# A depthwise convolution wholly on TensorE: four taps to a pass from shifted copies, four channel groups in the array's columns

## The chip, the core and the metric

The kernel runs on one core of a Trainium2 chip. Its time is the device time of one execution in microseconds (us). A core has TensorE (PE), VectorE (DVE), ScalarE (ACT), GpSimd (POOL) and SyncE (SP), which here only issues transfers. They run side by side and wait for one another through semaphores.

## What is computed

A sequence of 256 tokens of width 1024 and a context of as many go through two layers of four mixers (attention, Fourier, convolution, pooling), each followed by a gated FFN, and then through a second block. Both streams, sequence and context, pass layer 0's mixers; of the context, layer 1 needs keys and values only. The change touches the convolution, in each layer:

```python
def conv_module(a, dw_w, dw_b, ln_g, ln_b, w_pw):
    glu = a[..., :W_CONV] * jax.nn.sigmoid(a[..., W_CONV:])
    y = lax.conv_general_dilated(
        glu, dw_w[:, None, :], window_strides=(1,),
        padding=[(CONV_WIDTH // 2, CONV_WIDTH // 2)],
        dimension_numbers=('NWC', 'WIO', 'NWC'),
        feature_group_count=W_CONV) + dw_b
    y = jax.nn.silu(layer_norm(y, ln_g, ln_b))
    return y @ w_pw
```

with `W_CONV` 256 channels and `CONV_WIDTH` 31: each channel has its own 31 taps along the tokens.

## The kernel before

Channels lie on the partitions and tokens along the rows. Weights come in pieces of 128x1024 through a ring of four `raw` tiles on SP's queue (L232). ACT rounds each to `wh` (L244), DVE takes the rest as `wl` (L246), and a product is three passes on PE: `wh` by the high and low part of the activation `A`, and `wl` by the high part (`mm3`, L274 to L276; with tokens on the output's partitions `tm`, L299 to L301). A layer's input projections go in the order c (the convolution's input, two halves of 128 channels), Q, K/V, f (Fourier), p (pooling); attention, the mixers' small products and the output projection `p_wo` follow.

The program's order comes from a cooperative scheduler, `Flow`: side work is a generator that is spawned with a delay and yields estimated durations, and each piece of the main line calls `tick` with an estimate of its own, whereupon generators that have come due emit their next instructions. A list scheduler then orders each engine but SP by its estimates; SP keeps the program's order.

After `glu` has written the gated input to `GP` (L688; 15 zero columns on each side of each stream), the 31 taps of each half are shared out. `conv_pe` does 8 on PE: eight matmuls with a diagonal 128x128 matrix, `cdg`, over shifted views of `GP`, into the PSUM tile `p_cv`. `conv_taps` does 23 on DVE: L632, then 22 at L636, and L640 adds `p_cv`. `conv_ln` (layer norm, `p_mean`, `p_pw`) waits for both halves. N is 512 columns in layer 0 (two streams) and 256 in layer 1.

`mod_bg` streams the modulation matrices of later parts: for each piece POOL copies one element to `wm` (L422, which holds the load back until `pace[0]` is there), ACT issues the load (L423), and DVE does a weighted row sum for each stream (`jg` L427, `wm` L429). It starts when both `conv_taps` are done. The first two parts are done in the prologue by `p_mod` (L464), whose stationary operand is 128x32.

In attention, `p_s` at L763 is a score matmul, L740 its row minimum on DVE, `pe` (L743) the exponentials on ACT, `p_s` at L747 the transposes of these on PE, `pT` (L749) their copies, and `p_o` (L783) the product with V. `awo` is the output of a head group; L795 rounds it to `A` on ACT, L796 takes the rest on DVE. L948 adds `p_wo` to the residual `XC`. `p_ua` is the FFN's first product, whose input L364 and L365 write.

Of the kernel before, what the change touches and what calls it, by code (L numbers as in the profile page):

```python
# [24 lines left out]
F32 = mybir.dt.float32  # L25
# [6 lines left out]
D = 1024  # L32
# [6 lines left out]
GW = T + 2 * PAD  # L39
# [6 lines left out]
NPE = 8  # L46
CVD, FOD = 0.9, 1
# [58 lines left out]
for _n, _w in (("c", 16), ("bmod0", 48), ("bmod1", 48), ("g1_0", 8), ("g1_1", 8), ("g2_0", 8),  # L106
               ("g2_1", 8), ("dw_0", 62), ("dw_1", 62), ("db_0", 2), ("db_1", 2), ("lg_0", 2), ("lg_1", 2),
               ("lb_0", 2), ("lb_1", 2), ("ps_0", 2), ("ps_1", 2), ("n1", 8), ("n2", 8), ("fg", 8), ("bs", 8)):
    PK[_n] = _o
    _o += _w  # L110
# [42 lines left out]
def tile_kernel(ctx, tc, xin, pk_d, rows_d, lc_d, bc_d, wmod0, wmod, win, wout, wfi, wfo, wsm, win2w, win2, wproj, wout2,  # L153
# [30 lines left out]
    V.memset(ones, 1.0)  # L184
    mhalf = cpool.tile([128, 12], F32, name="mhalf")
# [9 lines left out]
    G.tensor_scalar(P("dw_0", 0, 124), P("dw_0", 0, 124), 0.5, None, op0=OP.mult)  # L195
# [367 lines left out]
    for l in range(2):  # L563
# [4 lines left out]
        with ExitStack() as mctx:  # L568
# [6 lines left out]
            UP = mp.tile([128, ns, UW], F32, name="UP")  # L575
            S2 = mp.tile([128, ns, UW], F32, name="S2")
            S4 = mp.tile([128, ns, UW], F32, name="S4")
            G.memset(UP[:, :, 0:POOL_PAD], 0.0)
            G.memset(UP[:, :, POOL_PAD + T:], 0.0)
            U = mp.tile([128, 2, N], F32, name="U")  # L580
# [4 lines left out]
            QT = [mp.tile([128, 2, 256], F32, name=f"QT{s}") for s in streams]  # L585

# [20 lines left out]
            cps = {}  # L607

            def conv_diag(f):

                w = lpool.tile([128, D], F32, tag="wm", name="cdg", bufs=WMB)
                for j in range(NPE):
                    tap = pk[:, PK[f"dw_{l}"] + f * TAPS + j:PK[f"dw_{l}"] + f * TAPS + j + 1]
                    if l == 0:
                        G.tensor_scalar(w[:, 128 * j:128 * j + 128], ident, tap, None, op0=OP.mult)
                    else:
                        S.activation(w[:, 128 * j:128 * j + 128], ident, AF.Copy, scale=tap)
                return w

            def conv_pe(f, w):  # L620

                cps[f] = psm("p_cv")
                for j in range(NPE):
                    PE.matmul(cps[f][:, :N].rearrange("p (s t) -> p s t", t=T), w[:, 128 * j:128 * j + 128],
                              GP[:, f, :, j:j + T], start=j == 0, stop=j == NPE - 1)
                    tick(0.0017 * N)

            def conv_taps(f, delay):
                y = Y[:, f].rearrange("p (s t) -> p s t", t=T)
                dw = PK[f"dw_{l}"] + f * TAPS  # L630
                per = 0.35 * ns
                V.tensor_scalar(y, GP[:, f, :, NPE:NPE + T], pk[:, dw + NPE:dw + NPE + 1], P(f"db_{l}", f), op0=OP.mult,  # L632
                                op1=OP.add)
                yield per + delay
                for j in range(NPE + 1, TAPS):
                    V.scalar_tensor_tensor(y, GP[:, f, :, j:j + T], pk[:, dw + j:dw + j + 1], y, op0=OP.mult, op1=OP.add)  # L636
                    yield per + delay
                while f not in cps:
                    yield 0.3
                V.tensor_tensor(Y[:, f], cps[f][:, :N], Y[:, f], op=OP.add)  # L640
                yield per
                G.tensor_copy(snap, Y[:, f, 0:1])
                pace[0] = snap
# [3 lines left out]
            def conv_ln(t0, t1):  # L647

                yield from wait(t0, t1)
# [86 lines left out]
            def att_unit(s, t, i, j, pT, sums, sp):  # L736
                nk = 4 if s == 0 else 2
                W = 128 * nk
                st = wk.tile([128, 1], F32, tag="ast", name="ast", bufs=4)
                V.tensor_reduce(st, sp[:, :W], axis=AX.X, op=OP.min)  # L740
                yield 0.8
                pe = mp.tile([128, 512], F32, tag="pe", name="pe", bufs=PEB)
                S.activation(pe[:, :W], sp[:, :W], AF.Exp, bias=st, scale=-1.0, accum_out=sums[:, j:j + 1])  # L743
                yield 0.9
                tp = sp
                for kt in range(nk):
                    PE.transpose(tp[:, 128 * kt:128 * kt + 128], pe[:, 128 * kt:128 * kt + 128], ident)  # L747
                yield 0.6
                S.copy(pT[:, :W], tp[:, :W])  # L749
                yield 0.5  # L750

            def attention(s, deps):
                yield from wait(*deps)
                nk = 4 if s == 0 else 2
                for t in range(2):
                    for i in range(2):
                        pts, us = [], []
                        sums = wk.tile([128, 2], F32, tag="asum", name="asum", bufs=4)

                        sps = [psm("p_s") for _ in range(2)]  # L760
                        for j in range(2):
                            pr = slice(64 * j, 64 * j + 64)
                            PE.matmul(sps[j][:, :128 * nk], QT[s][pr, t, 128 * i:128 * i + 128], KTt[pr, :128 * nk],  # L763
                                      start=True, stop=True)
                        yield 0.22 * nk + 0.2
                        for j in range(2):
                            pT = mp.tile([128, 512], F32, tag="PT", name="pT", bufs=PTB)
# [75 lines left out]

            PY = S2[:, :, POOL_PAD:POOL_PAD + T]

            def pool_f(f):
# [14 lines left out]
            def poolmix(f, d):  # L861
                yield d
                p = pmm("p_pl")
                PE.matmul(p[:, :N].rearrange("p (s t) -> p s t", t=T), sm[:, 1024 + 128 * f:1024 + 128 * f + 128], PY,
# [51 lines left out]
            for f in range(2):  # L916
                conv_pe(f, cdg[f])
# [539 lines left out]
def _pack(inp):  # L1457
# [9 lines left out]
    for l in range(2):  # L1467
# [3 lines left out]
        put(f"dw_{l}", inp["conv_dw_w"][l].reshape(TAPS, 2, 128).transpose(2, 1, 0).reshape(128, 2 * TAPS))  # L1471
# [79 lines left out]
```

## Time and profile before

| | us |
|---|---|
| median of 3 runs | 1340.57 (1340.22 to 1340.75) |
| the profiled execution | 1341.05 |
| its span | 1339.3 |

| engine | busy us | share of the span |
|---|---|---|
| PE | 1300.0 | 97% |
| DVE | 931.9 | 70% |
| ACT | 621.4 | 46% |
| POOL | 256.7 | 19% |

The span runs from the first to the last recorded instruction of the profiled execution; its own time is 1.75 us longer, and 0.48 us above the median. A matmul of f32 data shows as two records. Where it says fp32r, or where the operands are `wh`, `wl` and `A`, a matmul is one record. A record's duration includes the pipeline, so the spacing of starts tells what a matmul costs in a row of them. In the rows below, "128\*32" is the size of the stationary operand, "<-" stands between output and inputs, a bracket gives the idle time before an instruction and what ended it, and PEld is PE's weight loading.

### The profile page before, as it was taken

The page shows a single profiled execution, that of the slowest core. Times are in us where ns is not written, and L with a number is a line of the kernel's source. Part 1 is how long each engine was busy: PE and PEld are TensorE (multiplying, and loading weights), DVE is VectorE, ACT ScalarE, POOL GpSimd, SP SyncE. Part 2 cuts the span into 40 slices and gives each one's busy share as a digit, 9 for nine tenths or more (in the row PEclk, how much of TensorE's full clock was granted, in tenths as well). Part 3 has the DMA queues.
Part 4 walks back from the last instruction along what each step waited for, and adds up shares of the span by engine and source line. Part 5 has one row for each costly group of instructions (what it writes and reads, how often), then busy time and mean ns, then how long its engine had stood idle before and what let it go on. Part 6 is the DMA issues. An engine that isn't in the chain of part 4 may idle for free.

```text
span 1339.3 us, 20667 instructions
## 1 busy us (share of the span) xinstructions
PE 1300.0 (97%) x7764; PEld 1107.6 (83%) x7764; DVE 931.9 (70%) x1658; ACT 621.4 (46%) x1045; POOL 256.7 (19%) x310
## 2 busy tenths in 40 slices
PE   5999989899999999999999999999999999999997
PEld 4786569788888888899789999888788889888886
DVE  3697997999883333359667666657675777888754
ACT  4434534322132222245565554445675655655542
POOL 4134543243310000133420000010110002211100
PEclk9999999999999999999999999999999999999999
DMA  9624453677883222334135554675344344555463
GB/s 370 221 79 149 134 173 99 244 250 245 300 299 119 95 86 65 102 130 145 45 106 191 178 187 152 189 259 185 129 147 157 135 160 171 191 190 186 154 190 102
DMA packets 66612, 224.67 MB, mean 168 GB/s; under 512 B 7504, under 2 KB 8656, under 8 KB 66384
## 3 DMA queue, kind: packets, MB, share of 16 engines
q1 hardware_dynamic: 53968, 179.21, 39.8%
q10 hardware_dynamic: 12080, 42.50, 9.5%
q0 software_dynamic: 464, 1.64, 0.3%
q8 instruction: 61, 1.00, 0.3%
q14 instruction: 39, 0.32, 0.1%
HBM read 222.27 MB, written 1.05 MB: 167 GB/s over the span
## 4 chain that ended last, share of the span: by engine, by line
PE 87%; DVE 5%; DMA 2%; ACT 2%; issue 2%; POOL 1%; POOLq 0%; SPq 0%; DVEq 0%; ACTq 0%
PE p_dn L283 6%; PE p_ua L275 5%; PE p_ua L276 5%; PE p_ua L274 4%; PE p_ug L276 4%; PE p_ug L275 4%; PE p_ug L274 4%; PE p_ga L283 3%; PE p_gg L283 3%; PE p_dn L274 3%; PE p_dn L275 3%; PE p_dn L284 3%; PE p_dn L276 3%; PE p_gt L283 2%; PE p_wo L276 2%; PE p_wo L275 2%
## 5 line engine op out<-in xcount | busy, mean ns | idle before, releaser
L246 DVE TENSOR_TENSOR wl<-raw,wh 128x1024 fp32r<-128x1024 f32 (+2 forms) x340 | 393.6, 1159 | 249.2 <-ACT wh L244 247.7
L244 ACT CAST wh<-raw 128x1024 fp32r<-128x1024 f32 (+1 forms) x344 | 333.8, 974 | 317.9 <-PE p_ug L275 86.6
L339 POOL TENSOR_TENSOR ss<-ss,sq 128x256 f32<-128x256 f32 (+1 forms) x43 | 45.3, 1054 | 441.5 <-ACT sq L338 295.1
L275 PE MATMUL p_ua<-A,wh 128*128 128x258 f32 (+2 forms) x368 | 122.3, 332 | 3.5 <-DVE A L365 3.5
L283 PE MATMUL p_dn<-H,wh 128*128 128x512 f32 x352 | 124.1, 397 | 0.0
L276 PE MATMUL p_ug<-A,wl 128*128 128x258 f32 (+2 forms) x368 | 122.3, 332 | 0.0
L276 PE MATMUL p_ua<-A,wl 128*128 128x258 f32 (+2 forms) x368 | 122.1, 332 | 0.0
L275 PE MATMUL p_ug<-A,wh 128*128 128x258 f32 (+2 forms) x368 | 121.9, 331 | 0.0
L274 PE MATMUL p_ua<-A,wh 128*128 128x258 f32 (+2 forms) x368 | 121.6, 331 | 0.0
L274 PE MATMUL p_ug<-A,wh 128*128 128x258 f32 (+2 forms) x368 | 121.6, 331 | 0.0
L429 DVE SCALAR_TENSOR_TENSOR wm<-wm,scb 128x1024 f32<-128x1024 f32 x80 | 98.2, 1232 | 10.8 <-DMA wm<-in_wmod 10.7
L284 PE MATMUL p_dn<-H,wl 128*128 128x256 f32 x352 | 98.5, 281 | 0.0
L283 PEld LDWEIGHTS p_dn<-H,wh 128*128 128x128 f32 x352 | 66.0, 188 | 16.1
L275 PEld LDWEIGHTS p_ua<-A,wh 128*128 128x128 f32 x368 | 69.4, 189 | 11.0 <-DVE A L365 3.9
L275 PEld LDWEIGHTS p_ug<-A,wh 128*128 128x128 f32 x368 | 69.5, 189 | 7.2
L276 PEld LDWEIGHTS p_ua<-A,wl 128*128 128x128 f32 x368 | 69.5, 189 | 6.9
L274 PEld LDWEIGHTS p_ug<-A,wh 128*128 128x128 f32 x368 | 69.3, 188 | 7.0
L274 PEld LDWEIGHTS p_ua<-A,wh 128*128 128x128 f32 x368 | 69.3, 188 | 7.0
L276 PEld LDWEIGHTS p_ug<-A,wl 128*128 128x128 f32 x368 | 69.4, 189 | 6.9
L274 PE MATMUL p_dn<-H,wh 128*128 128x512 f32 (+1 forms) x198 | 72.4, 367 | 0.0
L275 PE MATMUL p_dn<-H,wh 128*128 128x512 f32 (+1 forms) x198 | 72.4, 366 | 0.0
L276 PE MATMUL p_dn<-H,wl 128*128 128x512 f32 (+1 forms) x198 | 72.4, 366 | 0.0
(380 smaller groups left out, 3130.4 us busy)
## 6 DMA issues: line engine op xcount, KB each, us to landing
raw<-in_wfi SPq DMA_DIRECT2D x88, 512.0 KB, 3.8
wm<-in_wmod ACTq DMA_DIRECT2D x80, 512.0 KB, 4.5
raw<-in_win SPq DMA_DIRECT2D x44, 512.0 KB, 3.8
raw<-in_wgu SPq DMA_DIRECT2D x44, 512.0 KB, 3.7
raw<-in_win2w SPq DMA_DIRECT2D x40, 512.0 KB, 4.0
raw<-in_wout SPq DMA_DIRECT2D x24, 512.0 KB, 3.7
raw<-in_wfo SPq DMA_DIRECT2D x32, 384.0 KB, 3.1
raw<-in_wfo SPq DMA_DIRECT2D x32, 320.0 KB, 3.2
```

The costliest lines, as they stand in the source:

```text
L244: S.copy(h[:, :n], raw[:, :n])
L246: (G if every and j % every == 0 else V).tensor_tensor(lo[:, :n], raw[:, :n], h[:, :n].bitcast(F32), op=OP.subtract)
L274: PE.matmul(ps, w[0], a[:, 0], start=first, stop=False, **kw)
L275: PE.matmul(ps, w[0], a[:, 1], start=False, stop=False, **kw)
L276: ins = PE.matmul(ps, w[1], a[:, 0], start=False, stop=last, **kw)
L283: PE.matmul(p.rearrange("p (h n) -> p h n", h=2), w[0], a, start=first, stop=False)
L284: PE.matmul(p[:, 0:256], w[1], a[:, 0], start=False, stop=last)
L339: (eng or G).tensor_tensor(ss[0][:, cs], ss[0][:, cs], sq[:, :n], op=OP.add)
L429: V.scalar_tensor_tensor(w, w, 1.0, scb[:, 0], op0=OP.mult, op1=OP.mult, accum_out=modv[:, l, part, 0, k:k + 1])
```

## The change

All taps go to PE, with a 32nd tap of zero. `conv_shift` copies each group of 32 channels of `GP` four times, shifted by 0 to 3 columns, to the four quarters of the partitions of `GS` (16 transfers a half, 32 a layer, 32 partitions by one or two streams by 284 columns each). A matmul with a 128x32 stationary matrix then adds four taps of 32 channels at once. `conv` does eight such passes for each of the four groups, 64 matmuls a layer; the four groups of a pass write the four quarters of `p_cv`'s partitions. ACT evacuates a half with the bias. `conv` is a generator, spawned 8.0 estimated us after `glu`; before, `conv_pe` stood on the main line behind K/V. `cdg` is now one broadcast product on POOL for each half. `mod_bg` waits for nothing any more; its first pieces are paced by `GP`. The tiles of the pooling mixer and of the exponentials (`UP`, `S2`, `S4`, `U`, `pe`, `pT`) are allocated when the convolution has been emitted, in the place of `GS`. Line numbers in the changed kernel are 3 higher up to the convolution; `p_cv` stands at L627, the copies at L618, and `jg` and `wm` at L430 and L432.

```diff
-NPE = 8
-CVD, FOD = 0.9, 1
+CVS = 8.0
+FOD = 1
...
+    id32 = cpool.tile([128, 32], F32, name="id32")
+    V.tensor_reduce(id32, ident.rearrange("p (g c) -> p c g", c=32), axis=AX.X, op=OP.add)
...
             def conv_diag(f):
-                w = lpool.tile([128, D], F32, tag="wm", name="cdg", bufs=WMB)
-                for j in range(NPE):
...
+                w = lpool.tile([128, D], F32, tag="wm", name="cdg", bufs=WMB).rearrange("p (q c) -> p q c", c=32)
+                G.tensor_tensor(w, id32[:, None, :].to_broadcast([128, 32, 32]),
+                                P(f"dw_{l}", 32 * f, 32)[:, :, None].to_broadcast([128, 32, 32]), op=OP.mult)
                 return w
...
+            def conv_shift(f):
+                gs = gp.tile([128, 4, ns, SW], F32, tag="GS", name="GS", bufs=2)
+                for g in range(4):
+                    for j in range(4):
+                        SP.dma_start(gs[32 * j:32 * j + 32, g], GP[32 * g:32 * g + 32, f, :, j:j + SW])
+                return gs
+
+            def conv(gss):
+                for f in range(2):
+                    p = psm("p_cv")
+                    for j in range(8):
+                        for g in range(4):
+                            PE.matmul(p[32 * g:32 * g + 32, :N].rearrange("p (s t) -> p s t", t=T), cdg[f][:, 4 * j + g],
+                                      gss[f][:, g, :, 4 * j:4 * j + T], start=j == 0, stop=j == 7)
+                        yield 0.35 * ns
+                    yield 0.4
+                    S.activation(Y[:, f], p[:, :N], AF.Identity, bias=P(f"db_{l}", f))
+                    yield 0.6
+                G.tensor_copy(snap, Y[:, 1, 0:1])
                 pace[0] = snap
...
-            cv0 = spawn(conv_taps(0, CVD))
-            cv1 = spawn(conv_taps(1, CVD), 0.5)
-            cv = spawn(conv_ln(cv0, cv1))
+            cvm = spawn(conv([conv_shift(f) for f in range(2)]), CVS)
+            cv = spawn(conv_ln(cvm))
             if l == 0:
+                pace[0] = GP[:, 1, 0, PAD:PAD + 1]
                 spawn(mod_bg([(0, 2, True, BG0), (0, 4, True, BG0), (0, 3, True, BG0), (0, 5, True, BG1),
                               (1, 1, True, BG1), (1, 0, True, BG1), (1, 2, False, BG1), (1, 4, False, BG1),
-                              (1, 3, False, BG1), (1, 5, False, BG1)], cv0, cv1))
+                              (1, 3, False, BG1), (1, 5, False, BG1)]))
...
-            for f in range(2):
-                conv_pe(f, cdg[f])
+
+            join(cvm)
+            gctx.close()
+            ap = mctx.enter_context(tc.tile_pool(name=f"a{l}", bufs=1))
...
```

On PE in layer 0, the convolution stood between the projections to f and p; the second half, and the start of the scores behind it, read like this before (`qt` is a rotated head, `ident` the identity with which PE transposes, `QT` and `KTt` the results):

```order
L276 MATMUL p_p<-A_73,wl 128x512
L727 MATMUL p_qt<-ident,qt_894 128x128 x3
L624 MATMUL p_cv<-GP,cdg 128x512 x8
L727 MATMUL p_qt<-ident,qt_923 128x128 x3
L763 MATMUL p_s<-KTt,QT_521 128x256 x4
L747 MATMUL p_s<-ident,pe 128x128 x4
L652 MATMUL p_mean<-Y,mean_w 128x512 x2
```

After, it stands among the K/V projections; here are the end of its first half and the start of its second:

```order
L302 MATMUL p_kv<-wh,A_73 128x256
L627 MATMUL p_cv<-GS,cdg 32x512 x29
L303 MATMUL p_kv<-wl,A_73 128x256
L304 MATMUL p_kv<-wh,A_73 128x256
L302 MATMUL p_kv<-wh,A_73 128x256
L303 MATMUL p_kv<-wl,A_73 128x256
L304 MATMUL p_kv<-wh,A_73 128x256
L627 MATMUL p_cv<-GS,cdg 32x512
L302 MATMUL p_kv<-wh,A_73 128x256
L303 MATMUL p_kv<-wl,A_73 128x256
L627 MATMUL p_cv<-GS,cdg 32x512
L304 MATMUL p_kv<-wh,A_73 128x256
```

The first three matmuls of each half are scattered singly among `p_kv` (those of the first half stand before this piece), and 29 follow in one run. In layer 1 the same engine has runs of 1, 1, 1, 30, 1, 1 and 29.

Behind the second run of 29, PE goes on with the scores of the first head:

```order
L277 MATMUL p_f<-A_73,wh 128x512
L627 MATMUL p_cv<-GS,cdg 32x512 x29
L754 MATMUL p_s<-KTt,QT_517 128x256 x2
L643 MATMUL p_mean<-Y,mean_w 128x512
L278 MATMUL p_f<-A_73,wh 128x512
```

From there 16 `p_f` matmuls, the other `p_mean` and three transposes stand ahead of the transposes of `pe`, which were next to the scores before.

On DVE, behind `glu` in layer 0, the row sums of `mod_bg` stand where the taps stood. Before (`qst` and `qt` belong to the Q/K preparation):

```order
L699 TENSOR_REDUCE qst<-qsq 128x6
L636 SCALAR_TENSOR_TENSOR Y<-GP,pk,Y 128x512 x2
L721 TENSOR_TENSOR qt_809<-QK_518,rows 128x256
L721 TENSOR_TENSOR qt_809<-QK_518,rows 128x128
L699 TENSOR_REDUCE qst<-qsq 128x6
L636 SCALAR_TENSOR_TENSOR Y<-GP,pk,Y 128x512 x2
L721 TENSOR_TENSOR qt_843<-QK_518,rows 128x256
```

and now:

```order
L690 TENSOR_REDUCE qst<-qsq 128x6
L432 SCALAR_TENSOR_TENSOR wm,modv<-wm,scb 128x1024
L712 TENSOR_TENSOR qt_891<-QK_514,rows 128x256
L712 TENSOR_TENSOR qt_891<-QK_514,rows 128x128
L690 TENSOR_REDUCE qst<-qsq 128x6
L430 SCALAR_TENSOR_TENSOR jg,modv<-wm,scb 128x1024
L712 TENSOR_TENSOR qt_936<-QK_514,rows 128x256
```

The Q/K preparation keeps its place among them; the tap operations are gone and the row sums, which came after the convolution, stand between its steps.

## Rows read from the trace of the kernel before

**Rows 1.** Page, busy time of each engine, share of the span, instructions
```profile
PE 1300.0 (97%) x7764; PEld 1107.6 (83%) x7764; DVE 931.9 (70%) x1658; ACT 621.4 (46%) x1045; POOL 256.7 (19%) x310
```

**Rows 2.** Page, the chain that ended last, shares of the span
```profile
PE 87%; DVE 5%; DMA 2%; ACT 2%; issue 2%; POOL 1%; POOLq 0%; SPq 0%; DVEq 0%; ACTq 0%
```

**Rows 3.** Stretches: length; busy PE, PEld, DVE, ACT, POOL; clock, DMA share, GB/s
```profile
56.60:112.70 56.10, 56.09 (x314) 44.81 (x314) 49.97 (x79) 15.63 (x33) 22.51 (x18) 1.00 0.25 81
112.70:195.30 82.60, 75.93 (x392) 49.63 (x391) 78.48 (x153) 42.18 (x103) 37.30 (x42) 0.98 0.55 179
...
593.70:646.50 52.80, 52.74 (x409) 51.12 (x409) 51.40 (x107) 25.96 (x56) 17.91 (x21) 1.00 0.40 132
646.50:696.80 50.30, 46.66 (x344) 38.48 (x344) 29.66 (x57) 32.31 (x69) 18.48 (x19) 1.00 0.21 68
```

**Rows 4.** Waits of PE, 50 to 260 us: total us, times, longest
```profile
PE p_ua L275 <- DVE A L365: 3.5, 2, 2.1
PE p_s L747 <- ACT pe L743: 1.9, 1, 1.9
PE p_wo L274 <- ACT A L795: 1.1, 1, 1.1
PE p_wo L274 <- DVE XC L948: 1.0, 1, 1.0
PE p_wo L275 <- DVE A L796: 1.0, 1, 1.0
```

**Rows 5.** Waits of PE, 585 to 720 us
```profile
PE p_s L763 <- DVE Y L640: 1.2, 1, 1.2
...
PE p_o L783 <- ACT pT L749: 1.0, 1, 1.0
```

**Rows 6.** Groups of instructions, DVE taps of layer 0: busy us, mean ns | idle
```profile
L636 DVE SCALAR_TENSOR_TENSOR Y<-GP,pk,Y 128x512 f32<-128x512 f32 x44 | 31.4, 753 | 0.0
```

**Rows 7.** Timeline of PE: start, duration in us, instruction
```profile
105.87 7.04 PE L624 MATMUL p_cv<-GP,cdg 128*128 128x512 f32 x16
112.75 0.49 PE L727 MATMUL p_qt<-ident,qt 128*128 128x128 f32 x3
```

**Rows 8.** Groups of instructions, convolution matmuls of layer 1
```profile
L624 PE MATMUL p_cv<-GP,cdg 128*128 128x256 f32 x32 | 7.2, 379 | 0.0
```

**Rows 9.** Timeline of PE around one modulation piece of the prologue
```profile
33.32 0.39 PE L275 MATMUL p_c<-A,wh 128*128 128x512 f32 x1
33.55 0.39 PE L276 MATMUL p_c<-A,wl 128*128 128x512 f32 x1
33.87 1.93 PE L464 MATMUL p_mod<-rawm,scf 128*32 128x256 f32 x32
35.74 0.50 PE L274 MATMUL p_c<-A,wh 128*128 128x512 f32 x1
36.08 0.39 PE L275 MATMUL p_c<-A,wh 128*128 128x512 f32 x1
```

**Rows 10.** Timeline of SP's DMA issues
```profile
50.42 0.33 SPq L571 DMA_DIRECT2D sm<-in_wsm  x1
51.87 7.57 SPq L232 DMA_DIRECT2D raw<-in_win  x4
```

**Rows 11.** Timeline of DVE, second half of `GP` in layer 0
```profile
59.47 0.68 DVE L688 SCALAR_TENSOR_TENSOR GP<-sg,p_c 128x512 f32<-128x512 f32 x1
```

**Rows 12.** DMA issues: size, median us from issue to landing
```profile
pk<-in_pk SPq DMA_DIRECT2D x1, 8.0 KB, 2.0
```

**Rows 13.** Stretch of attention, line 427 alone: DVE busy, clock, DMA share, GB/s
```profile
112.70:195.30 82.60, 28.93 (x44) 0.98 0.55 179
```

**Rows 14.** Timeline of DVE in the tail of layer 0's attention
```profile
190.65 1.22 DVE L427 SCALAR_TENSOR_TENSOR jg<-wm,scb 128x1024 f32<-128x1024 f32 x1
...
191.80 0.29 DVE L796 TENSOR_TENSOR A<-awo,A 128x128 fp32r<-128x128 f32 x1
```

**Rows 15.** Groups of instructions, weight loads of the convolution matmuls
```profile
L624 PEld LDWEIGHTS p_cv<-GP,cdg 128*128 128x128 f32 x64 | 11.7, 189 | 7.0 <-issue 6.3
```

More of the change, by code (lines that the diff above doesn't have):

```diff
@@ L38 @@
 PAD = 15
-GW = T + 2 * PAD
+GW = T + 2 * PAD + 1
+SW = T + 28
 POOL_PAD = 8
@@ L106 @@
 for _n, _w in (("c", 16), ("bmod0", 48), ("bmod1", 48), ("g1_0", 8), ("g1_1", 8), ("g2_0", 8),
-               ("g2_1", 8), ("dw_0", 62), ("dw_1", 62), ("db_0", 2), ("db_1", 2), ("lg_0", 2), ("lg_1", 2),
+               ("g2_1", 8), ("dw_0", 64), ("dw_1", 64), ("db_0", 2), ("db_1", 2), ("lg_0", 2), ("lg_1", 2),
                ("lb_0", 2), ("lb_1", 2), ("ps_0", 2), ("ps_1", 2), ("n1", 8), ("n2", 8), ("fg", 8), ("bs", 8)):
@@ L192, in P @@
         return pk[:, PK[name] + i:PK[name] + i + n]
-    G.tensor_scalar(P("dw_0", 0, 124), P("dw_0", 0, 124), 0.5, None, op0=OP.mult)
+    G.tensor_scalar(P("dw_0", 0, 128), P("dw_0", 0, 128), 0.5, None, op0=OP.mult)
     seq = []
@@ L574, in tile_kernel @@
             G.memset(GP[:, :, :, PAD + T:], 0.0)
[L575 to L580, printed above, removed]
             Y = mp.tile([128, 2, N], F32, name="Y")
@@ L585, in tile_kernel @@
             QT = [mp.tile([128, 2, 256], F32, name=f"QT{s}") for s in streams]
+            gctx = mctx.enter_context(ExitStack())
+            gp = gctx.enter_context(tc.tile_pool(name=f"g{l}", bufs=1))
             CG = mp.tile([128, 2, 2, 64], F32, name="CG")
@@ L606, in tile_kernel @@
             acc = {}
-            cps = {}
             def conv_diag(f):
-                w = lpool.tile([128, D], F32, tag="wm", name="cdg", bufs=WMB)
-                for j in range(NPE):
[L613 to L617, printed above, removed]
-                return w
@@ L620, in conv_pe @@
[L620 to L642, printed above, removed]
+                w = lpool.tile([128, D], F32, tag="wm", name="cdg", bufs=WMB).rearrange("p (q c) -> p q c", c=32)
@@ L643, in conv_taps, with conv_ln @@
                 pace[0] = snap
             in_done = []
-            def conv_ln(t0, t1):
-                yield from wait(t0, t1)
+            def conv_ln(t0):
+                yield from wait(t0)
                 mean = psm("p_mean")
@@ L741, in att_unit @@
                 yield 0.8
-                pe = mp.tile([128, 512], F32, tag="pe", name="pe", bufs=PEB)
+                pe = ap.tile([128, 512], F32, tag="pe", name="pe", bufs=PEB)
                 S.activation(pe[:, :W], sp[:, :W], AF.Exp, bias=st, scale=-1.0, accum_out=sums[:, j:j + 1])
@@ L766, in attention @@
                         for j in range(2):
-                            pT = mp.tile([128, 512], F32, tag="PT", name="pT", bufs=PTB)
+                            pT = ap.tile([128, 512], F32, tag="PT", name="pT", bufs=PTB)
                             pts.append(pT)
@@ L842, in fourier @@
                 yield 1.5
-            PY = S2[:, :, POOL_PAD:POOL_PAD + T]
             def pool_f(f):
@@ L854, in pool_f @@
                     G.tensor_tensor(S4[64:, :, 8:w - 7], S2[64:, :, 4:w - 11], S2[64:, :, 12:w - 3], op=OP.add)
+                PY = S2[:, :, POOL_PAD:POOL_PAD + T]
                 cnt = lc[:, LC_CNT + 256 * f:LC_CNT + 256 * f + 256]
@@ L863, in poolmix @@
                 p = pmm("p_pl")
-                PE.matmul(p[:, :N].rearrange("p (s t) -> p s t", t=T), sm[:, 1024 + 128 * f:1024 + 128 * f + 128], PY,
+                PE.matmul(p[:, :N].rearrange("p (s t) -> p s t", t=T), sm[:, 1024 + 128 * f:1024 + 128 * f + 128],
+                          S2[:, :, POOL_PAD:POOL_PAD + T],
                           start=True, stop=True)
@@ L915, in tile_kernel @@
             done(n_, 3)
-            for f in range(2):
-                conv_pe(f, cdg[f])
+            join(cvm)
+            gctx.close()
+            ap = mctx.enter_context(tc.tile_pool(name=f"a{l}", bufs=1))
+            UP = ap.tile([128, ns, UW], F32, name="UP")
+            S2 = ap.tile([128, ns, UW], F32, name="S2")
+            S4 = ap.tile([128, ns, UW], F32, name="S4")
+            G.memset(UP[:, :, 0:POOL_PAD], 0.0)
+            G.memset(UP[:, :, POOL_PAD + T:], 0.0)
+            U = ap.tile([128, 2, N], F32, name="U")
             at = []
@@ L1470, in _pack @@
         put(f"g2_{l}", _fm(inp["g_norm2"][l]))
-        put(f"dw_{l}", inp["conv_dw_w"][l].reshape(TAPS, 2, 128).transpose(2, 1, 0).reshape(128, 2 * TAPS))
+        dw = np.concatenate([inp["conv_dw_w"][l].reshape(TAPS, 256), np.zeros((1, 256), np.float32)])
+        put(f"dw_{l}", dw.reshape(8, 4, 2, 4, 32).transpose(1, 4, 2, 0, 3).reshape(128, 64))
         for n, s in (("db", "conv_dw_b"), ("lg", "conv_ln_g"), ("lb", "conv_ln_b"), ("ps", "pool_scale")):
```

## The prediction

> **What bounds the kernel now.** I read the page first: TensorE is busy for 97% of the span [rows 1], and the chain that ended last is 87% PE, 5% DVE [rows 2]. So a change pays only where PE stands idle, and costs wherever it adds PE time. Next the table of stretches [rows 3], which separates the places. While layer 0 projects Q, K/V, f and p and convolves (56.6 to 112.7), PE is busy 56.09 of 56.10 us and DVE 49.97: the 23 taps on DVE are wholly hidden. The attention stretch behind it (112.7 to 195.3) has 82.60 - 75.93 = 6.67 us of PE idle and a granted clock of 0.98. Layer 1 has the same pair: 52.74 of 52.80 busy, then 50.30 - 46.66 = 3.64 idle. The list of PE's waits says on whom: in layer 0 1.9 us on the exponentials `pe` (ACT), 1.1 on ACT's `A`, 1.0 on DVE's `A`, 1.0 on DVE's `XC`, and 3.5 on DVE's `A` in the norm before the FFN, behind the attention stretch [rows 4]; in layer 1 1.2 on `Y` L640 and 1.0 on `pT` [rows 5].
>
> **What the DVE taps were worth.** 44 operations of 753 ns, 31.4 us, leave DVE in layer 0 [rows 6], fewer and shorter ones in layer 1. All lies in stretches where PE waits for nothing, so the removal itself gains 0. The work that covers it is PE's own projections; without that cover it would cost its 31 us.
>
> **What the convolution costs on PE.** Before, an f32 matmul of 128x512 is two records; 16 records last from 105.87 to 112.75, 6.88 us, so 0.43 a record and 0.86 a matmul [rows 7]; layer 0 has 16 matmuls. In layer 1, 256 columns, 32 records are busy 7.2 us [rows 8]; start to start I take half of 0.43, thus 0.43 a matmul. After, a layer has 64 matmuls with a 128x32 stationary, four to a pass in different columns of the array. Whether four share the time of one decides all. The nearest row is the modulation in the prologue: 128\*32 stationary, 256 columns, also in four column groups; 32 records in 1.93 us [rows 9]. One after another they would need 32 x 0.215 = 6.9; four abreast 8 x 0.215 = 1.72. So they run side by side, and 16 full passes of four cost what the 16 matmuls cost before.
>
> But the order does not give full passes. In layer 0 the first three matmuls of each half stand alone among the `p_kv` matmuls, which use the whole array; the other 29 come in one piece. 29 over four groups are 8 waves, so a half takes 3 + 8 = 11 waves instead of 8: 22 against 16, + 6 x 0.86 = 5.2 us. Layer 1 goes 1, 1, 1, 30, 1, 1, 29, where 30 and 29 take 8 waves each: 21 against 16, + 5 x 0.43 = 2.1. Together +7.3. This is the surest term; its bounds are 6.5 and 8.
>
> Each piece also goes from whole-array to four-group use and back. The modulation prices it: its neighbours start at 33.55 and 36.08, 2.53 apart; the two ordinary matmuls in that stretch take 0.23 each (33.32 to 33.55), and 2.53 - 0.46 - 1.72 leaves 0.35; with 7.2 / 32 = 0.225 a record it leaves 0.27 [rows 8, 9]. I take 0.3. There are 8 pieces in layer 0 and 7 in layer 1: 15 x 0.3 = 4.5 us; bounds 0 (if the leftover is the modulation's weight loads alone) and 15 x 0.35 = 5.3.
>
> [...] PE total: +11.8.
>
> **The shift copies.** SP issues the four `raw` halves until 51.87 + 7.57 = 59.44, an issue takes 0.33 [rows 10]; the second half of `GP` is written at 59.47 + 0.68 = 60.15 [rows 11]. The 32 copies are issued behind, 10.6 us of SP. The nearest transfer, `pk` of 8 KB, lands 2.0 after its issue [rows 12]. So the first 16 land by 59.4 + 5.3 + 2 = 66.7, all by 72. PE starts Q at 56.6 and meets the first convolution matmul 99 matmuls of 256 columns later (half of 0.23 each, 11.4): 68. The second half comes after 154 of them, 11 waves and some switches: near 85. So no wait, with 1 us to spare at first and 13 later; what is queued behind the copies on SP, `in_wout`, is wanted only after attention. Cost 0; the bound above is in the rivals.
>
> **What becomes of the waits.** In layer 0 `mod_bg` no longer waits for the convolution and starts near 60 instead of 114. Before, 22 of its loads (44 rows, each operation with the read of its accumulator) ran in the 82.6 us of attention [rows 13], 3.75 us a load. 24 loads need 90 us, so they end near 150, and the tail of attention no longer has them. That tail shows what they cost: `jg` starts at 190.65 for 1.22 us, and `A`, for which PE waits, right behind it at 191.80 [rows 14]; `XC` stands behind two more of them. So the two DVE waits of 1.0 go. The `pe` wait of 1.9 goes as well, since `p_mean` and 16 `p_f` matmuls now stand between the scores and their transposes on PE. ACT's `A` (1.1) follows the last head and stays. Of the remaining 6.67 - 5.0 = 1.67 and of the clock's 0.02 x 82.6 = 1.65 I count half each, 0.8 and 0.8, because part of `mod_bg` is still there. Layer 0 saves 1.9 + 2.0 + 0.8 + 0.8 = 5.5. The 3.5 before the FFN stays: the loads of part (0,5) still stand between the norm's DVE operations, as the unchanged row order there shows. In layer 1 the wait on L640 (1.2) goes with its instruction, and of the other 2.44 I count half: 2.4. Saved: 7.9. Bounds: 3.2 (only the three waits on named DVE operations) and 6.67 - 1.1 + 1.65 + 3.64 = 10.9 (all but ACT's `A`).
>
> **Small edits at nothing.** The taps' matrices become one POOL operation a half, the identity sum one DVE operation; both are built long before use. ACT evacuates `Y` twice a layer while PE has `p_f` to do. `U`, `UP` and the pools that reuse the copies' space wait for the last convolution matmul, but the `p_f` results that fill `U` come after it on PE anyway. Early `mod_bg` puts 20 operations of 1.2 us on DVE where about 33 us of taps were, and its transfers meet a DMA share of 0.25 [rows 3]. Should the Q/K preparation slip behind them, p_f still covers; bound 1.5 us.
>
> **The sum.** 1341.05 (the profiled execution: span 1339.3 and 1.75 around it) + 7.3 + 4.5 - 7.9 = 1344.95. That execution lies 0.48 above the median 1340.57, so I predict **1344.5 us**. Bounds of the terms: 6.5 + 0 - 10.9 = -4.4 (1336) and 8 + 5.3 + 1.5 - 3.2 = +11.6 (1352).
>
> **Rivals.**
> *Faster: DVE's relief reaches further.* For: DVE is busy 78.48 of 82.60 us in the attention stretch [rows 3], and everything that PE waits for there passes through DVE or ACT. If all idle but ACT's `A` goes, the norm's 3.5 with it, and switching is free: 7.3 - 10.9 - 3.5 = -7.1, 1333.5. It decides once savings pass 7.3 + 2.7 = 10.0 with free switching, or 14.5 at 0.3. Against: the norm's rows stand as they did.
> *Late copies.* If the 32 copies land one after another instead of beside each other, each takes 0.33 + 2.0: the second half is there at 59.4 + 75 = 134 instead of 85, up to 49 us lost; with half the margin, some 10 us: 1354 and up. For: 32 small transfers with a wait each, the `GP` write as late as 60.15, and a spare of 1 us at first. Against: transfers overlap everywhere in this trace.
> *Groups that do not share.* If each of a pass's weight loads had to wait for the running matmul, every wave of records would carry one load of 0.19 [rows 15]: 43 waves x 2 x 0.19 = 16.3 us more, 1361. Against: the modulation has at most 0.35 left over for 8 waves.
> [...]
> *Little happens.* The early `mod_bg` gains and PE's added waves cancel: savings of 10, costs of 10, within 2.7 us of before.
>
> **How the numbers follow.** 0.2%, 2.7 us, is about what a measurement of this kernel can tell from no change. The forecast (1341 to 1349, waves and switches paid, waits partly gone) 0.6, of it 0.48 slower by more than 2.7 and 0.12 within; little happens or slightly faster than that 0.15 (0.12 within, 0.03 faster); faster 0.12; late copies 0.09; groups that do not share 0.04. Thus faster 0.15, same 0.24, slower 0.61. The range 1337 to 1353 leaves out most of the last three.
>
> **What would show it.** In the changed trace: 29 `p_cv` matmuls lasting near 8 x 0.86 = 6.9 us, single ones 0.86 plus 0.3; no PE wait on a copy; 15 pieces; PE's waits on `XC` and on `A` L796 gone, `mod_bg` through its first 24 loads by 150; the waits before the FFN and on ACT's `A` as before. Wrong would make it: 29 that last 10 us or more, a wait ahead of `p_cv`, or a new wait of the transposes on DVE's `ast` minimum behind `jg`.

## The result, and the profile after

The changed kernel takes 1353.78 us (median of 4 runs, 1352.22 to 1355.1) against 1340.66 before: a ratio of 1.0098, 95% interval 1.0085 to 1.011. The prediction was 1344.5 us, at most 1353. The sign was right and the size was not: 13 us slower instead of 4. The profiled execution has a span of 1353.0 us, 13.7 more than before.

Where the 13.7 us lie is read from one table, whose stretches begin at the first `p_q`, at the first `p_ua`, and at the first `p_c`, `p_q` and `p_ua` of layer 1. In the kernel before (length, PE busy, granted clock, DMA share, GB/s):

```profile
56.60:219.50 162.90, 156.21 (x908) 0.99 0.40 131
219.50:593.70 374.20, 369.31 (x1771) 1.00 0.51 172
593.70:606.60 12.90, 12.84 (x105) 1.00 0.52 172
606.60:696.80 90.20, 86.56 (x649) 1.00 0.28 91
696.80:1339.30 642.50, 633.22 (x4030) 1.00 0.52 171
```

and of the changed kernel:

```profile
56.60:229.70 173.10, 167.31 (x1002) 0.97 0.44 137
229.70:604.00 374.30, 369.61 (x1770) 1.00 0.52 172
604.00:619.60 15.60, 14.53 (x104) 0.89 0.52 168
619.60:711.60 92.00, 90.58 (x743) 1.00 0.31 98
711.60:1353.00 641.40, 632.32 (x4030) 1.00 0.52 172
```

Layer 0 from Q to the FFN is 10.2 us longer, the start of layer 1 2.7, layer 1's mixers 1.8, the rest 1.0 shorter. A stretch splits into idle time (length minus busy), clock loss (busy time times one minus the clock, read from stretches of 4 us, since this table rounds the clock) and work (the remainder). Layer 0: idle 6.69, now 5.79; clock loss 1.7, now 5.1; work 154.5, now 162.2, so +7.7. Layer 1's mixers: idle 3.64, now 1.42; work +4.0.

The waits of PE in layer 0 of the changed kernel, the answer to [rows 4]:

```profile
PE p_ua L278 <- DVE A L368: 3.4, 2, 2.1
PE p_pl L854 <- POOL S L849: 2.6, 2, 2.1
PE p_cv L627 <- DMA GS<-GP: 1.6, 1, 1.6
PE p_wo L277 <- ACT A L786: 1.0, 1, 1.0
PE p_o L774 <- ACT pT L740: 0.3, 1, 0.3
PE p_s L738 <- ACT pe L734: 0.2, 1, 0.2
```

The two DVE waits of the tail are gone, the one on `pe` has shrunk from 1.9 to 0.2, `A` on ACT and the wait before the FFN have stayed: all as predicted. Two are new: the pooling product `p_pl` waits for POOL, and the first convolution matmul for a copy. The convolution matmuls themselves (timeline of PE; each is two records):

```profile
70.05 1.02 PE L627 MATMUL p_cv<-GS,cdg 128*32 128x512 f32 x2 [1.56 <-DMA GS<-GP]
...
71.92 0.28 PE L303 MATMUL p_kv<-wl,A 128*128 128x256 f32 x1
72.13 1.05 PE L627 MATMUL p_cv<-GS,cdg 128*32 128x512 f32 x2
73.11 0.39 PE L304 MATMUL p_kv<-wh,A 128*128 128x256 f32 x1
73.33 0.28 PE L302 MATMUL p_kv<-wh,A 128*128 128x256 f32 x1
...
80.02 7.05 PE L627 MATMUL p_cv<-GS,cdg 128*32 128x512 f32 x58
```

The run of 29 (58 records) lasts 7.05 us: 8 waves of 0.86 and the tail of the last. A single one costs 73.33 - 71.92 = 1.41 from the neighbour ahead to the one after next; those two take 0.24, so 1.17: 0.86 and 0.31 more, which comes with each piece of 128x32 matmuls between 128x128 ones. The other single ones give the same, those of layer 1 with 0.43 in place of 0.86.

Had each record waited for one weight load of 0.19 us [rows 15], the 8 waves would have taken 8 x 2 x 0.19 = 3.0 us more; 7.05 us leaves no room for that here.

What follows the new wait on POOL is in the stretches of 4 us around it (busy PE, PEld, DVE, ACT, POOL; clock, DMA share, GB/s):

```profile
140.00:144.00 4.00, 2.08 (x11) 1.60 (x10) 3.48 (x6) 1.06 (x4) 3.92 (x4) 1.00 0.00 0
144.00:148.00 4.00, 3.47 (x14) 2.70 (x14) 3.29 (x6) 4.00 (x11) 0.52 (x2) 0.73 0.84 280
148.00:152.00 4.00, 4.00 (x18) 2.57 (x17) 4.00 (x8) 1.64 (x6) 3.86 (x4) 0.50 0.44 141
152.00:156.00 4.00, 4.00 (x9) 1.69 (x8) 4.00 (x6) 1.04 (x4) 3.85 (x3) 0.50 0.69 241
```

PE stands idle for some 2 us while DVE and POOL are full; then the clock granted to TensorE is 0.73 from 144 to 148 and 0.50 until 156: 0.27 x 4 + 0.5 x 8 = 5.1 us, twice the idle time around the wait (1.92 + 0.53 from 140 to 148). Before, the drop in the same place cost (0.11 + 0.32) x 4 = 1.7:

```profile
140.00:144.00 4.00, 3.11 (x15) 1.31 (x13) 4.00 (x12) 2.47 (x4) 3.85 (x5) 0.89 0.41 158
144.00:148.00 4.00, 4.00 (x11) 1.82 (x9) 4.00 (x6) 1.92 (x5) 3.92 (x2) 0.68 0.02 7
```

The pooling that PE waits for had been early before. Its first half ran on POOL (L848 to L859) ahead of the first row sum of `mod_bg`, and its product on PE came 23 us later (the last row is PE's):

```profile
106.41 1.30 POOL L848 TENSOR_TENSOR S<-UP 128x542 f32<-128x542 f32 x1 [0.26 <-ACT UP L937]
...
111.82 1.27 POOL L859 TENSOR_TENSOR S<-S,UP 128x512 f32<-128x512 f32 x1
...
135.94 1.02 PE L864 MATMUL p_pl<-S,sm 128*128 128x512 f32 x2
```

In the changed kernel the first `p_p` starts at 117.2 instead of 98.2 and ACT copies the result of the first half to `UP` at 131.39 instead of 105.75, so this chain begins 26 us later, among the row sums, while its product is due only 6 us later than before.

### The profile page after: what moved, and what is told of

Read it like the earlier page. It is cut to its first block, busy times and chain, and to the rows that moved or that the text cites. A ratio compares the mean times of both kernels' runs of the same rounds, so it can differ in the third digit from the quotient of the medians.

```text
span 1353.0 us, 21038 instructions
## 1 busy us (share of the span) xinstructions
PE 1317.1 (97%) x7956; PEld 1109.3 (82%) x7956; DVE 887.3 (66%) x1563; ACT 618.2 (46%) x1033; POOL 240.4 (18%) x296
## 3 DMA queue, kind: packets, MB, share of 16 engines
HBM read 222.27 MB, written 1.05 MB: 165 GB/s over the span
## 4 chain that ended last, share of the span: by engine, by line
PE 87%; DVE 4%; DMA 3%; POOL 3%; issue 2%; ACT 1%; POOLq 0%; DVEq 0%; SPq 0%; ACTq 0%
PE p_dn L286 6%; PE p_ua L278 5%; PE p_ua L279 5%; PE p_ua L277 5%; PE p_ug L279 5%; PE p_ug L278 5%; PE p_ug L277 4%; PE p_ga L286 3%; PE p_gg L286 3%; PE p_dn L277 3%; PE p_dn L278 3%; PE p_dn L279 3%; PE p_dn L287 3%; PE p_gt L286 2%; DMA wm<-in_wmod 2%; PE p_wo L277 2%
## 5 line engine op out<-in xcount | busy, mean ns | idle before, releaser
L432 DVE SCALAR_TENSOR_TENSOR wm<-wm,scb 128x1024 f32<-128x1024 f32 x80 | 102.2, 1282 | 9.0 <-DMA wm<-in_wmod 8.2
L430 DVE SCALAR_TENSOR_TENSOR jg<-wm,scb 128x1024 f32<-128x1024 f32 x48 | 61.7, 1286 | 18.1 <-DMA wm<-in_wmod 18.1
```

Of the source, the lines that this page charges most:

```text
L430: V.scalar_tensor_tensor(jg, w, 1.0, scb[:, 1], op0=OP.mult, op1=OP.mult, accum_out=modv[:, l, part, 1, k:k + 1])
L432: V.scalar_tensor_tensor(w, w, 1.0, scb[:, 0], op0=OP.mult, op1=OP.mult, accum_out=modv[:, l, part, 0, k:k + 1])
```

## The experiments

Theory 1: the eight unexplained microseconds of layer 0 come from `mod_bg`, whose loads and row sums, started early, meet the Q/K preparation, the pooling and the exponentials. Rival: they come from the convolution's new place, which puts off everything behind it.

**The convolution late.**

```diff
-CVS = 8.0
+CVS = 22.0
```

> The convolution's generator is spawned 22.0 instead of 8.0 estimated us after glu, so that its matmuls come in unbroken runs of 32, 32 and 64 and stand behind the K/V projection. Both theories: 11 waves fewer (7.3 us), 12 changes of array mode fewer (3.6 us) and no wait for the copies (1.6 us), 12.5 us below the changed kernel. Theory 1 (the PE wait of 2.6 us on the pooling chain and the clock drop behind it come from mod_bg's loads, which now run in the same stretch): they stay, 1341 us. Rival (they come from the convolution's place ahead of f and p, which makes the pooling late): they go too, 6 to 7 us more, 1335 us.

Measured 1350.76 us, 1.0074 (1.0057 to 1.0091): only 3 of the 12.5 us. Layer 1's mixers took 84.7 us instead of 92.0 and were wholly busy. Of these 7.3 us 1.4 were idle time; `p_cv` and its neighbours `p_kv` and `p_f`, from start to start, take 24.2 instead of 28.1, and 3.9 is what 5 waves and 6 pieces were counted for; the other 2.0 lie mostly in the attention matmuls and `p_wo` and were not counted. In layer 0 the work fell by some 5 us to 157, where 7 had been counted, and PE waited elsewhere:

```profile
PE p_qt L718 <- DVE qt L713: 8.6, 3, 4.1
PE p_s L738 <- ACT pe L734: 3.4, 2, 3.0
```

TensorE ran at half clock (0.50 granted) for 10 us from 108 and for 10 from 152, each time around a gap; counted where PE was busy, that cost 7.7 us. What follows: neither theory as put; the figures were missed by 10 and 16 us. Without the early convolution the Q/K preparation queued behind the row sums on DVE: the trouble is not at the pooling chain alone.

**`mod_bg` early, alone** (the kernel before):

```diff
+                pace[0] = GP[:, 1, 0, PAD:PAD + 1]
                 spawn(mod_bg([
...
-                              (1, 3, False, BG1), (1, 5, False, BG1)], cv0, cv1))
+                              (1, 3, False, BG1), (1, 5, False, BG1)]))
```

> The kernel before, with only mod_bg's start moved to right behind glu. Theory 1: the row sums and the taps compete on DVE, and the pooling chain on POOL has the markers of mod_bg between its steps: PE waits on one of them, 1343 to 1350 us. Rival: without the convolution's new place there is no such wait and the two DVE waits in attention's tail go, 1338 to 1339 us.

Measured 1377.3 us, 1.0274 (1.0259 to 1.029). The rival falls. The mechanism is Theory 1's in kind (row sums and taps compete on DVE), in another place and far dearer than expected: one wait of 17.6 us, and 44 us of layer 0 at half clock (0.50 granted), 20 of them idle.

```profile
PE p_qt L727 <- DVE qt L722: 17.6, 1, 17.6
```

**The convolution alone** (the changed kernel, `mod_bg` held back as before):

```diff
-                pace[0] = GP[:, 1, 0, PAD:PAD + 1]
...
-                              (1, 3, False, BG1), (1, 5, False, BG1)]))
+                              (1, 3, False, BG1), (1, 5, False, BG1)], cvm))
```

> The changed kernel, but mod_bg waits for the convolution as it did before. Theory 1: mod_bg then starts near 107 us and is in the pooling's stretch as well; the pooling wait stays and the two waits of 1.0 us in attention's tail come back: 1354 to 1358 us. Rival: the same wait, for another reason; the tail's 2 us more. If it is faster than the changed kernel by over 3 us, mod_bg's early start itself did the harm.

Measured 1350.71 us, 1.007 (1.0055 to 1.0085), 3.1 us under the changed kernel and outside Theory 1's range. Here another result was late (`p_fa` waited 3.2 us for ACT), and the lower clock beside it (0.75 and 0.82 granted from 140 to 148) cost 1.5 us instead of 5.1. The wait on the copies is gone. The tail's two waits did not come back, against the expectation. So the early start did no good, and the late one is not free of collisions. The change still costs 10 us here: 12 of PE's work in the mixers of both layers, 3.5 of idle time saved there, and the start of layer 1 2.7 longer.

**Without the first 24 loads** of `mod_bg` (constants for these parts):

```diff
         for l, part, with_ctx, gap_ in parts:
+            if (l, part) in ((0, 2), (0, 3), (0, 4)):
+                G.memset(modv[:, l, part], 1.0)
+                mods.add((l, part))
+                continue
```

> The changed kernel without the first three parts of mod_bg (24 loads, their markers, their row sums; constants in their place, so the output differs). Theory 1: the wait on the pooling chain and the clock drop in 140 to 160 go: 6 to 8 us below the changed kernel, 1345 to 1348 us. Rival (the place of the convolution): wait and drop stay, within 2 us of the changed kernel but for two waves fewer, 1351 to 1353 us.

Measured 1340.72 us, 1.0003 (0.9987 to 1.0018): 13 us below the changed kernel, more than expected. Layer 0 has no idle time and no clock loss at all, and the wait on the copies is gone too:

```profile
55.50:215.10 159.60, 159.60 (x1002) 1.00 0.23 69
```

The convolution stands in its new place here, so that place alone makes no wait. But the pooling is late here too (`UP` at 127.22); its chain takes 6.3 us, and 6.7 are left before its product. What the rival says of the place is thus part of the cause, as far as the traces show: it leaves the pooling a reserve of 5 to 7 us (6.7 here, 5.2 with short sums, below), and the row sums, which lengthen the chain by 5.7, use that up. No run has the early convolution with an early pooling. **The same in the kernel before**, as the counterpart:

> The kernel before without the first three parts of mod_bg, constants in their place: the counterpart to the changed kernel without them (1340.72 us). Theory 1: before's waits of 6.7 us and clock loss of 1.6 in layer 0 mostly go: 1332 to 1335 us, so that the difference between the two, 6 to 9 us, is the waves and pieces that the scattered matmuls add on PE. Rival (the old kernel's waits came from its taps on DVE): 1338 to 1341 us.

Measured 1336.51 us, 0.9971 (0.9961 to 0.9981). With the loads out of both, the new convolution costs 1340.72 - 1336.51 = 4.2 us; with them in, 13.1. So some 9 of the 13 us come with the loads, and the old kernel had paid 4 for them. In layer 0 the loads cost the changed kernel 13.5 us (5.8 idle, 5.1 clock, 2.6 of PE work, since without them the convolution's matmuls stand in 20 waves instead of 22) and the old one 4.9. The measured time lies between the two expectations.

**Both edits, and a third start.** Late convolution with `mod_bg` behind it, and late convolution with `mod_bg` behind the Q/K preparation (`prepared` is a generator that waits for it; `CVS` is 22.0 in both):

```diff
...
-                              (1, 3, False, BG1), (1, 5, False, BG1)]))
+                              (1, 3, False, BG1), (1, 5, False, BG1)], spawn(prepared())))
```

> Both edits: the convolution's generator 22.0 after glu (unbroken runs of 32, 32 and 64 matmuls) and mod_bg waiting for it as before the change. Theory 1 (the harm is mod_bg's loads meeting the Q/K preparation and the pooling chain; the convolution itself, unbroken, costs PE nothing over the old one): layer 0 needs 154 us of PE work as in the late convolution plus some 8 us of waits and clock as before, layer 1's mixers 85 instead of 90 us: 1335 us, 1332 to 1338. Rival (a convolution on PE makes something else late by itself): 1341 us or more.

> The late convolution, with mod_bg waiting for the Q/K preparation instead of nothing. Theory 1: the waits of p_qt on DVE (8.6 us in the late convolution) and their clock drop go, a wait on the pooling chain may stay: 1334 to 1342 us. Rival: as the late convolution, near 1350 us.

Measured 1349.14 us (1.0062, 1.0047 to 1.0077) and 1340.87 (1.0001, 0.9992 to 1.0011). The first misses Theory 1's figure by 14 and lies where the rival had put it: layer 1 gave its 5.5 us, but layer 0 had 10.9 us of waits, on ACT, DVE and POOL, none of them over 2.6, and 7.6 of clock loss. The second is as fast as the kernel before, since layer 0 is 6 us longer and layer 1 as much shorter. Its edit held back less than it was to: the sums of the first three loads still ran from 67 to 77 us, the others from 109.

**What of the loads does the harm.** The row sums over 64 of 1024 columns (the modulation differs); the other operation is shortened in the same way:

```diff
...
-                V.scalar_tensor_tensor(w, w, 1.0, scb[:, 0], op0=OP.mult, op1=OP.mult,
+                V.scalar_tensor_tensor(w[:, :64], w[:, :64], 1.0, scb[:, 0, :64], op0=OP.mult, op1=OP.mult,
```

> The changed kernel with mod_bg's row sums over 64 of 1024 columns (the modulation then differs); its loads, markers and queues stay. If DVE's time is what delays the chains: layer 0 as without the first loads, 1339 to 1344 us. If it is the loads that stand in ACT's queue and the markers in POOL's, or the transfers: a wait of 2 us or more and a clock drop stay, 1347 to 1354 us. In both the rest of the kernel gains little, since later row sums are hidden.

Measured 1348.38 us, 1.0069 (1.0042 to 1.0096). The time lies in the range of the loads and queues; the sign that was to go with it, a long wait and a fall of the clock in layer 0, is absent. Layer 0 took 163.2 us instead of 173.1, with 3.0 idle, 2.2 of it on the copies, and the clock whole; 2.1 of the 9.9 are PE work, since here too the convolution has 20 waves. The stretches around 144:

```profile
140.00:144.00 4.00, 4.00 (x18) 2.50 (x17) 1.93 (x5) 2.91 (x7) 0.00 (x0) 1.00 0.44 129
144.00:148.00 4.00, 4.00 (x26) 2.47 (x26) 3.91 (x8) 1.96 (x7) 2.75 (x3) 1.00 0.38 85
148.00:152.00 4.00, 4.00 (x16) 2.21 (x15) 2.59 (x7) 2.54 (x8) 3.77 (x4) 1.00 0.12 48
```

The harm near 140 us is the length of the row sums, not the transfers. Nor is it the standing of a queue as such: in layer 0 ACT still stood 15.6 us before loads that waited for their markers (25.8 in the changed kernel, 3.9 before the change), and DVE 23.7 us before sums that waited for their loads (15.7 in the changed kernel), and PE did not stop for it. (The first FFN took 3.7 us longer in that execution, which hid part of the gain.) What the sums do to POOL is seen in the pooling chain. In the changed kernel:

```profile
131.03 1.24 POOL L437 TENSOR_TENSOR modv<-modv,pk 128x8 f32<-128x8 f32 x1
132.23 2.07 POOL L837 TENSOR_TENSOR S<-UP 128x542 f32<-128x542 f32 x1
...
136.07 2.14 POOL L847 TENSOR_TENSOR S<-S,lc 64x512 f32<-64x512 f32 x1
138.17 1.18 POOL L440 TENSOR_TENSOR modv<-modv,pk 128x8 f32<-128x8 f32 x1
...
142.00 1.18 POOL L425 COPY wm<-snap 128x1 f32<-128x1 f32 x1
143.13 1.26 POOL L849 TENSOR_TENSOR S<-S,UP 128x512 f32<-128x512 f32 x1
```

and with short sums:

```profile
131.84 0.20 POOL L437 TENSOR_TENSOR modv<-modv,pk 128x8 f32<-128x8 f32 x1 [6.81 <-DVE jg L430]
132.30 1.09 POOL L837 TENSOR_TENSOR S<-UP 128x542 f32<-128x542 f32 x1 [0.26 <-ACT UP L936]
...
134.78 2.60 POOL L847 TENSOR_TENSOR S<-S,lc 64x512 f32<-64x512 f32 x2
137.47 1.29 POOL L849 TENSOR_TENSOR S<-S,UP 128x512 f32<-128x512 f32 x1
```

The chain takes 12.2 us beside long sums and 6.5 beside short ones, as it took 6.7 before the change, when it ran ahead of `mod_bg` (the second half met the sums before as well and took 12.6, but its product on PE was not due sooner); a sum of 8 columns takes 1.24 instead of 0.20. It goes both ways: beside the pooling a row sum lasts up to 2.29 instead of 1.22 (DVE in the changed kernel):

```profile
137.01 2.28 DVE L430 SCALAR_TENSOR_TENSOR jg<-wm,scb 128x1024 f32<-128x1024 f32 x1
...
139.96 2.03 DVE L432 SCALAR_TENSOR_TENSOR wm<-wm,scb 128x1024 f32<-128x1024 f32 x1
...
141.92 1.22 DVE L430 SCALAR_TENSOR_TENSOR jg<-wm,scb 128x1024 f32<-128x1024 f32 x1
```

0.20 becomes 1.24, 1.04 more, where a row sum lasts 1.22. What makes each slow the other was not shown.

**Slower pacing.** The first three parts at 4.0 instead of 2.4 in the changed kernel, and at 3.2 in the version with `mod_bg` behind the preparation:

```diff
-BG0, BG1 = 2.4, 2.0
+BG0, BG1 = 4.0, 2.0
```

> The changed kernel with mod_bg's first three parts paced at 4.0 instead of 2.4 estimated us a load; all else as changed. Theory: DVE is less crowded between 60 and 150 us, the wait on the pooling chain and the clock drop behind it shrink, 4 to 8 us below the changed kernel, 1346 to 1350 us. Rival (order by chance): within 3 us of the changed kernel or above it.

> The late convolution with mod_bg after the Q/K preparation, and mod_bg's first three parts paced at 3.2 instead of 2.4 estimated us a load. Theory (DVE's row sums crowd the chains that feed PE in layer 0; fewer of them at a time leave gaps): layer 0 falls from 168.8 us to 158 to 164, 1330 to 1337 us. Rival (the waits come from the order that the scheduler happens to choose, not from the density): layer 0 changes by either sign, 1336 to 1348 us.

Measured 1354.86 us (1.0101, 1.0087 to 1.0115) and 1341.9 (1.0005, 0.9996 to 1.0014): no gain. In the changed kernel 13 row sums `jg` stand between 105 and 160 us with either pace. Spreading by the estimate does not thin the sums where they hurt.

**The pooling product later on PE.**

```diff
...
-                    po.append(spawn(poolmix(0, 0.0)))
+                    po.append(spawn(poolmix(0, 12.0)))
...
```

> The changed kernel with the first pooling product p_pl some 15 rows later on PE (its generator delayed by 12.0 estimated us); the second half of the pooling uses the dead GP instead of S2, so that it need not wait for the first product. The convolution's matmuls and mod_bg stand as in the changed kernel. Theory: the wait of 2.1 us on the pooling chain goes, and with the gap the fall of the clock behind it, some 5 us: layer 0 166 to 169 us, 1346 to 1350 us. Rival 1 (the clock falls there for another reason than the gap): only the 2.1 to 2.6 us go, 1351 us. Rival 2 (the exponentials and the Fourier results are late as well): the wait moves to the next instruction, 1352 to 1356 us.

Measured 1352.63 us, 1.0094 (1.0075 to 1.0113). Rival 2 holds: the wait moves on, to the transposes of `pe`.

```profile
PE p_s L738 <- ACT pe L734: 2.7, 1, 2.7
...
PE p_pl L855 <- POOL GP L850: 1.4, 1, 1.4
```

ACT had stood 2.95 us in front of a `mod_bg` load that waited for its marker on POOL:

```profile
141.31 0.34 ACTq L426 DMA_DIRECT2D wm<-in_wmod  x1
141.75 1.04 ACT L247 CAST wh<-raw 128x1024 fp32r<-128x1024 f32 x1 [2.95 <-POOL wm L425]
```

**The small POOL instructions of `mod_bg` on DVE**, to see whether that detour is the cause:

```diff
-                G.tensor_copy(w[:, 0:1], pace[0])
+                V.tensor_copy(w[:, 0:1], pace[0])
...
```

and so for the three small sums behind.

> The changed kernel with mod_bg's small POOL instructions (the markers and the sums with the bias, 8 columns) on DVE; loads, row sums and pacing stay. If the detour over POOL is the cause: the stop near 140 us and the fall of the clock go, layer 0 from 173 to 163 to 167 us, 1343 to 1348 us. If DVE's time for the row sums is: a stop of 2 us or more stays within 135 to 160 us, 1350 to 1356 us.

Measured 1358.64 us, 1.0142 (1.0122 to 1.0162), above both ranges: the detour is not the cause. The stop stayed and grew, on DVE directly (PE waited 3.2 us for `awo`, 1.7 for `U`, 0.9 for `asum`).

> The late convolution with mod_bg after the Q/K preparation (1340.87 us) and mod_bg's small POOL instructions on DVE. Detour over POOL: layer 0 from 168.8 to 158 to 163 us, 1331 to 1336 us. DVE's time: within 3 us of 1341.

Measured 1343.18 us, 1.0022 (1.0012 to 1.0032): the same answer.

**Layer 1 only.** The kernel before, with the change in layer 1 alone, the generator spawned at 22.0:

```diff
...
+            if l == 0:
                 cv0 = spawn(conv_taps(0, CVD))
                 cv1 = spawn(conv_taps(1, CVD), 0.5)
                 cv = spawn(conv_ln(cv0, cv1))
+            else:
+                cvm = spawn(conv([conv_shift(f) for f in range(2)]), CVS)
+                cv = spawn(conv_ln(cvm))
...
```

> Layer 0 and mod_bg as before the change; in layer 1 the convolution wholly on PE, spawned 22.0 after glu, so in one run of 64. Theory: nothing competes in layer 1 (no mod_bg there), its mixers take 84.7 us as in the late convolution instead of 90.2: 1335 to 1336 us, faster than both. Rival (the gain in layer 1 hung on what came before it): 1339 to 1341 us.

Measured 1337.9 us, 0.998 (0.9972 to 0.9989), faster than both kernels (0.2% under the one before) and between the two expectations. The mixers of layer 1 are without a gap:

```profile
609.30:695.20 85.90, 85.90 (x745) 1.00 0.36 109
```

85.9 instead of 90.2 us, of which 3.6 had been idle; in this execution the first FFN took 2.4 us more. With `mod_bg`'s small instructions on DVE as well:

> Layer 0 as before the change, the late convolution in layer 1 only (1337.9 us), and mod_bg's small POOL instructions on DVE. Detour over POOL: layer 0 from 162.8 to 157 to 160 us, 1333 to 1336 us. DVE's time: 1336 to 1340 us.

Measured 1334.39 us, 0.9959 (0.9945 to 0.9973), the fastest here. Not for the reason expected: layer 0 did not become shorter (164.2 us), but the stretch of the first FFN did (371.6 instead of 374.2 before), as PE's 3.5 us on the norm's `A` shrank to 1.1 on the FFN's first evacuation.

## Why the prediction was wrong

By its own steps:

- **The cost on PE held.** Forecast +7.3 for waves and +4.5 for pieces, 11.8; measured 7.7 + 4.0 = 11.7 of work, and a piece costs 0.31, not 0.3. The passes of four share the time of one: 29 matmuls of 128x32 took 7.05 us, the 8 of 128x128 before 6.88.
- **The shift copies were not free.** The prediction took 0.33 us an issue and 2.0 to land from an 8 KB transfer. Here 13 of them take 12.67 us of SP's queue, and one lands 3.8 after its issue:

```profile
59.46 12.67 SPq L618 DMA_DIRECT2D GS<-GP  x13
GS<-GP SPq DMA_DIRECT2D x32, 71.0 KB, 3.8
```

 PE waited 1.6 us for the first group, where 1 us of margin had been counted; the second half was there in time. With `mod_bg`'s loads left out or held back the wait did not occur; it was 1.2 to 2.2 us in the five versions that have both the early loads and the early convolution: the prediction had not counted that the copies meet these loads.
- **The step that failed is the one on the waits**, "saved: 7.9, bounds 3.2 to 10.9". The waits named there did go. But layer 0's idle time without the copies fell only from 6.7 to 4.2, and its clock loss rose from 1.7 to 5.1 instead of halving: layer 0 lost 0.9 us where 5.5 were to be saved. Layer 1 saved 2.2 of 2.4. In all 1.3 saved instead of 7.9, below the lower bound. The reasoning took away waits and added none. It counted the row sums by their sum on DVE (20 operations where taps had been), not by what stands behind each of them, nor by how much they and POOL slow each other. And it put the pooling at nothing ("`p_f` results that fill `U` come after it on PE anyway"), when the results that fill `UP` now came 26 us later. Nor was the end of the loads right: 90 us were counted, and the last `jg` of this group ends near 169, not 150. 13 us of that are a pause from 97 to 110: only the first ten loads are paced by `GP`, the markers of the others copy `snap`, which waits for the convolution.
- **The start of layer 1** was not in the sum: 15.6 instead of 12.9 us, 1.7 of it clock (0.89 granted) and 0.8 a wait of `p_q` for ACT's `sg`. In the other versions it was 12.8 to 15.6, and 14.5 or more wherever the clock fell there, behind the same wait of 1.4 us that all have. That is not bound to the early convolution: two of the late ones have it, and two early ones with the loads in do not. Its cause was not settled.
- **The rest** is 1.0 us shorter. So 3.9 became 3.9 + 6.6 + 1.6 + 2.7 - 1.0 - 0.1 = 13.7.
- **The rivals.** Late copies: the mechanism, at a sixth of its price. Groups that do not share: excluded (7.05 us for 8 waves). DVE's relief: the opposite.

That the row sums on DVE are needed for the stop near 140 us is shown: it goes with the loads left out or the sums shortened, and stays when the pacing, the pooling product or the markers are moved. That the late pooling is needed as well for the wait of the changed kernel is read from the two traces (22.9 us of reserve before, none after) and was not tested alone; where pooling, pacing or markers were moved, PE stopped for other late results instead. That the clock falls because of the gap is only seen together: near 140 us every version with a gap of 2 us or more had the fall, the kernel before had it after 0.9 us, and those without a gap (loads out, sums shortened) had none. But the change in layer 1 alone had a gap of 1.1 us there and no fall; a gap of 1.9 us (on `pe`, before the change) passed without one; and the wait of 2.1 us before the FFN was followed by one in the changed kernel without the first loads (0.97 granted from 200 to 260 us) and in neither of the two kernels (1.00). So the size of the gap alone does not settle it, nor the price: near 140 us a gap of 3.2 us (`mod_bg` held back) cost 1.5 us of clock, one of 2.1 (slower pacing) 8.1.

## What to carry to other kernels

Taking work off an engine gains only the waits that hang on it, and what the freed time is then filled with can cost much: ask what stands behind the new work in each engine's queue, not whether its sum fits. When a piece of work moves to another place on the critical engine, ask also what it puts off there, and how much reserve that had. Count the clock behind a gap of PE as well: here 2.5 us of idle time were followed by 5.1 us of clock loss. And look at each place of a change alone: layer 1's part, which was free of other side work, was a gain (4.3 us in its stretch, 1337.9 us in all), and layer 0's ate it.

## What the runs showed of the hardware

POOL instructions of 1 or 8 columns took 1.05 to 1.24 us instead of 0.2 beside DVE's row sums of 128x1024, and these up to 2.29 instead of 1.22 us beside the pooling. Each piece of 128x32 matmuls between 128x128 ones cost 0.31 us beyond its waves, of 0.86 us each at 512 columns. SBUF-to-SBUF copies of 71 KB over 32 partitions went out at about 1 us each on one queue and landed 3.8 us after their issue beside `mod_bg`'s loads, 36 KB ones, in layer 1, 1.9.
